# Transformer layer on one core: the last memory product, the first half's sums, the ahead products and the turned rows become steps of the planned list, and eight pairs run ahead

## The chip, the cores and the metric

One core of one Trainium2 chip runs the kernel. Its engines are named as the profile names them: PE (TensorE, matrix products and transposes, which are products with the identity), DVE (VectorE), ACT (ScalarE), POOL (GpSimd), SP (SyncE, which issues most DMAs). The metric is the device time of one execution in microseconds; less is better.

## The reference

One layer on 1024 rows of 1024 features in float32: two attention groups with an output projection, attention into 256 memory rows, and a feed forward with squared ReLU, each with an RMS norm before and after it and a residual sum. The parts around the change, cut from the reference:

```python
h = rmsnorm(x, g_mem_pre[l])
...
y = memory_cross_attention(h, mem_n, w_mq[l], w_mk[l], w_mv[l], w_mo[l])
x = x + rmsnorm(y, g_mem_post[l])
h = rmsnorm(x, g_ff_pre[l])
y = jnp.square(jax.nn.relu(h @ w_ff1[l])) @ w_ff2[l]
x = x + rmsnorm(y, g_ff_post[l])
```

`memory_cross_attention` ends with `o @ w_mo`; these are the memory products below.

## The kernel before

**How numbers are kept.** Each float32 operand of a product is split into a hi piece (a copy in a narrower form, made on ACT) and a lo piece (the rest, made by a subtraction on DVE or POOL). `mm3` (line 172) makes one product from three matmuls: hi by hi (L174), lo by hi (L175), hi by lo (L176). A weight block is thus loaded (SP), copied (ACT, L336), subtracted (DVE, L341, or POOL, L344) and only then used.

**How products are tiled.** A large product over two by two blocks is made from seven block products and sums of blocks. For the memory output the seven are listed in `MO` (L210); the last has the name A22. Each is made for two halves of the rows (rows 0 to 3 and rows 4 to 7, a row being 128 rows of x), in two pieces of weights (kp) and for two rows (tp). Their results are added in `ym` (`leave`, L1642), multiplied by the gain g_mem_post, normed and added to x (`close_row`, L1152: the inverse root `rm` on POOL, L1122 and L1123, then the close on DVE, L1163). The feed forward makes 16 pairs of blocks of hidden features (NP), each pair by seven products: `px`, `py`, `pz`, `pv`. The first half's rows, turned, are h3T; the second half's rows are turned on PE (trx, L2096), and sums and differences of the two halves, T1 to T4, are formed with B22 (class `Turn`, L2082).

**What sets the order.** Up to L1949 a planner, `Flow` (L56), issues the work. Streams of steps for PE are tried in a fixed order; a step is taken when its condition holds, and its cost moves a modelled clock. Work for the other engines is put into a list for each engine with the earliest time, a cost and a level; of what can start, the lowest level goes first. `Stock` (L269) puts the loads and splits of weight blocks into the same lists, up to some blocks ahead. The planner runs while the kernel is built; on the chip each engine takes its instructions in the order so made, and an instruction that waits holds all that stand behind it on that engine.

From L1966 on the order is written out by hand: the eight sums `xf` of hi and lo pieces of h3T on POOL (L2076), the loads and splits of the first blocks of w_ff1 (`split_ahead`, L2052), the second half's A22 product (L2172 on), the closes of its rows 6 and 7 (`row_out`, `row_sum`), four units of transposes and sums (`units[...].turn()`, `.sums()`, `.low()`), and between them the ahead products: for AHEAD = 7 pairs the first row, px and py, which need the first half's rows alone (`ahead`, L2060). Their results go to DRAM (p1d) and are read again when the pair's turn comes in the loop over the 16 pairs (`reload`). Just ahead of the loop stand the block sums of pair 0 (`cur.sums`, L2228 to L2235) and the splits of them, v0 and s1a.

## Time and profile before

| | before |
|---|---|
| median of 3 runs | 1468.5 us |
| lowest, highest | 1467.78 us, 1469.2 us |
| the profiled execution | 1469.17 us |
| its span | 1467.4 us |
| mean granted PE clock in it | 0.994 |

The times agree within 1.4 us. The span is that from the first to the last instruction of the profiled execution; its own time is 1.8 us longer. Rows of the profile give a line of the kernel, the operation, and "out<-in" by the program's names without numbers: `ym<-whimo,A22h` is a matmul of the last memory product, `trx<-ident,ym` a transpose of the second half's rows, `xf<-h3T_hi,h3T_lo` one of the eight sums. The time in square brackets is that for which the engine stood before the instruction, with what released it.

### The profile page before, as it was taken

The page shows a single profiled execution, that of the slowest core. Times are in us where ns is not written, and L with a number is a line of the kernel's source. Part 1 is how long each engine was busy: PE and PEld are TensorE (multiplying, and loading weights), DVE is VectorE, ACT ScalarE, POOL GpSimd, SP SyncE. Part 2 cuts the span into 40 slices and gives each one's busy share as a digit, 9 for nine tenths or more (in the row PEclk, how much of TensorE's full clock was granted, in tenths as well). Part 3 has the DMA queues.
Part 4 walks back from the last instruction along what each step waited for, and adds up shares of the span by engine and source line. Part 5 has one row for each costly group of instructions (what it writes and reads, how often), then busy time and mean ns, then how long its engine had stood idle before and what let it go on. Part 6 is the DMA issues. An engine that isn't in the chain of part 4 may idle for free.

```text
span 1467.4 us, 20996 instructions
## 1 busy us (share of the span) xinstructions
PE 1437.7 (98%) x7188; PEld 1213.0 (83%) x7188; DVE 980.7 (67%) x1678; ACT 865.8 (59%) x1542; POOL 474.5 (32%) x515
## 2 busy tenths in 40 slices
PE   9999999999999999999999699999999999999997
PEld 9888888888889978888787588888888888888886
DVE  5567778868677436785879787765555656655576
ACT  7457776667577755577787565545555443444442
POOL 1345555445435361343444703343232000000021
PEclk9999999999999999999999899999999999999999
DMA  8234677954546884454346557764444785345565
GB/s 332 72 94 103 137 171 180 278 127 111 130 111 190 275 311 158 146 199 129 130 130 201 183 201 250 246 217 158 152 149 166 282 320 182 137 152 189 189 241 201
DMA packets 102699, 268.89 MB, mean 183 GB/s; under 512 B 12968, under 2 KB 25520, under 8 KB 102592
## 3 DMA queue, kind: packets, MB, share of 16 engines
q1 hardware_dynamic: 97840, 259.16, 53.0%
q0 software_dynamic: 4608, 8.39, 3.9%
q8 instruction: 56, 0.92, 0.3%
q14 instruction: 51, 0.42, 0.1%
q10 hardware_dynamic: 144, 0.00, 0.0%
HBM read 187.23 MB, written 80.27 MB: 182 GB/s over the span
## 4 chain that ended last, share of the span: by engine, by line
PE 87%; DVE 4%; DMA 3%; ACT 2%; POOL 2%; issue 1%; SPq 0%; DVEq 0%; POOLq 0%; ACTq 0%
PE fx L176 4%; PE pv L654 4%; PE fx L174 4%; PE fx L175 4%; PE ptr L604 4%; PE px L174 3%; PE px L175 3%; PE px L176 3%; PE fy L176 3%; PE fy L174 3%; PE fy L175 3%; PE q L174 2%; PE q L175 2%; PE q L176 2%; PE pz L174 2%; PE pz L175 2%
## 5 line engine op out<-in xcount | busy, mean ns | idle before, releaser
L610 DVE TENSOR_TENSOR p<-ptr,p 128x512 fp32r<-128x512 f32 (+1 forms) x152 | 92.3, 616 | 32.5 <-ACT p L613 31.4
L2453 POOL TENSOR_SCALAR rf<-sf,e 128x1 f32<-128x1 f32 x8 | 8.6, 1069 | 323.9 <-ACT jf L2438 323.9
L2339 ACT ACTIVATE whif<-ra 128x1024 fp32r<-128x1024 f32 x37 | 39.3, 1061 | 125.4 <-PE fy L175 62.6
L613 ACT ACTIVATE p<-ptr 128x512 fp32r<-128x512 f32 (+1 forms) x152 | 79.7, 538 | 43.7 <-PE ptr L604 42.8
L2341 DVE TENSOR_TENSOR wlof<-ra,whif 128x1024 fp32r<-128x1024 f32 x37 | 45.3, 1225 | 88.0 <-ACT whif L2339 88.0
L654 PE MATMUL pv<-p,vs 128*128 128x512 f32 (+1 forms) x304 | 86.2, 371 | 0.4 <-DVE p L610 0.4
L2228 POOL TENSOR_TENSOR sc<-wf,wf 128x512 f32<-128x512 f32 x14 | 20.9, 1493 | 143.7 <-DMA wf<-in_w_ff 95.3
L174 PE MATMUL fx<-vhif,whif 128*128 128x512 f32 x168 | 65.4, 389 | 0.0
L176 PE MATMUL fx<-vhif,wlof 128*128 128x512 f32 x168 | 65.4, 389 | 0.0
L175 PE MATMUL fx<-vlof,whif 128*128 128x512 f32 x168 | 65.4, 389 | 0.0
L654 PEld LDWEIGHTS pv<-p,vs 128*128 128x128 f32 x304 | 53.0, 189 | 8.8 <-DVE p L610 0.8
L174 PE MATMUL k<-hT_hi,whik 128*128 128x512 f32 x128 | 52.8, 412 | 0.0
L174 PE MATMUL yw<-whiwo,yT_hi 128*128 128x512 f32 x128 | 50.4, 394 | 0.7 <-ACT yw L1215 0.7
L174 PE MATMUL q<-hT_hi,whiq 128*128 128x512 f32 x128 | 51.0, 398 | 0.0
L176 PE MATMUL k<-hT_hi,wlok 128*128 128x512 f32 x128 | 50.3, 393 | 0.0
L175 PE MATMUL k<-hT_lo,whik 128*128 128x512 f32 x128 | 50.2, 392 | 0.0
L175 PE MATMUL q<-hT_lo,whiq 128*128 128x512 f32 x128 | 50.1, 391 | 0.0
L176 PE MATMUL q<-hT_hi,wloq 128*128 128x512 f32 x128 | 50.0, 391 | 0.0
L176 PE MATMUL yw<-whiwo,yT_lo 128*128 128x512 f32 x128 | 49.9, 390 | 0.0
L175 PE MATMUL yw<-wlowo,yT_hi 128*128 128x512 f32 x128 | 49.8, 389 | 0.0
L174 PE MATMUL fy<-vhif,whif 128*128 128x512 f32 x128 | 49.8, 389 | 0.0
L175 PE MATMUL fy<-vlof,whif 128*128 128x512 f32 x128 | 49.8, 389 | 0.0
(740 smaller groups left out, 5078.1 us busy)
## 6 DMA issues: line engine op xcount, KB each, us to landing
ra<-gd SPq DMA_DIRECT2D x56, 512.0 KB, 3.5
wg<-in_w_ff SPq DMA_DIRECT2D x56, 512.0 KB, 4.7
wf<-in_w_ff SPq DMA_DIRECT2D x38, 512.0 KB, 4.1
gd<-s SPq DMA_DIRECT2D x48, 256.0 KB, 2.1
od<-ot SPq DMA_DIRECT2D x64, 128.0 KB, 2.9
od<-od POOLq DMA_DIRECT2D x32, 256.0 KB, 5.2
wrawmo<-wtT SPq DMA_DIRECT2D x16, 512.0 KB, 3.4
gd<-u SPq DMA_DIRECT2D x32, 256.0 KB, 2.4
```

Source lines behind the costliest of these rows:

```text
L174: nc.tensor.matmul(ps, lh, rh, start=start, stop=False, skip_group_check=more)
L175: nc.tensor.matmul(ps, lh, rl, start=False, stop=False, skip_group_check=more)
L176: nc.tensor.matmul(ps, ll, rh, start=False, stop=stop, skip_group_check=more)
L604: nc.tensor.transpose(tr[:, m, :], sp[:, k * P:(k + 1) * P], ident)
L610: flow.put("V", at, 0.56 if dead else 0.7, lambda: nc.vector.tensor_sub(pl[:, live, :], tr[:, live, :], f(ph[:, live, :])), done)
L613: flow.put("S", flow.end, 0.49 if dead else 0.6, lambda ph=ph, tr=tr, live=live: nc.scalar.activation(ph[:, live, :], tr[:, live, :], AF.C ...
L654: nc.tensor.matmul(pv[:, :, q0 * P:(q0 + k1 - k0) * P], v, x[:, :, k0:k1, :].rearrange("p m k q -> p m (k q)"), start=c == 0 and m == 0, s ...
L2228: eng.tensor_sub(sc[:, k1], r0[:, k0], r1[:, k0])
L2339: nc.scalar.activation(ah, ra, AF.Copy)
L2341: nc.vector.tensor_sub(al, ra, f(ah))
L2453: nc.gpsimd.tensor_scalar(r, ssf[b][:, 0:1], ssf[b][:, 1:2], e3[:, b:b + 1], op0=ALU.add, op1=ALU.add)
```

## The change

The list that `Flow` runs now reaches to the loop over the pairs. `product_quarters` makes all seven products for both halves. The sums `xf` are put into POOL's list at its last level, once h3T is complete and the attention's outputs are done. The ahead products of pairs 0 to 5 are steps of the stream of products (`first_rows`, named pf), their weights are blocks of `Stock`, and the transposes with their sums are a stream of their own (`unit_steps`, `unit`). AHEAD becomes 8; pairs 6 and 7 are still written by hand behind the list, with the last lows of T3 and T4 and the splits of pair 0. The hi pieces of mo and ff weights are put at ACT's first level. The four multiplications by the gain in each half that POOL did are done by DVE. The block sums of pair 0 go from DVE to POOL, and `Rows` loads the residual rows of all eight rows.

```diff
+            self.blocks += [(("ff", j), t["w_ff1"][j].rearrange("p a b -> p (a b)"), [P, D]) for j in range(8)]
...
+            self.home.update({("ff", j): "w" if j > 5 else ("w", "wq")[j % 2] for j in range(8)})
...
+                        flow.put(eng, at, 1.22, lambda: self.lo(key, e), last, 0 if key[0] in ("mo", "ff") else 1)
...
-                flow.put("S", flow.now, 1.06, lambda key=key: self.hi(key), halves, 2)
+                flow.put("S", flow.now, 1.06, lambda key=key: self.hi(key), halves, 0 if key[0] in ("mo", "ff") else 2)
...
-            self.left = [("w", n) for n in range(TB)] + [("m", n) for n in range(6)]
+            self.left = [("w", n) for n in range(TB)] + [("m", n) for n in range(8)]
...
-        for p, (a, _) in enumerate(MO[:7 - th]):
+        for p, (a, _) in enumerate(MO):
...
-        if th:
-            lasts.append(X)
...
-                flow.chain(at, [("S", 0.65, square(y[:, cs])), ("G", 1.6, lambda: nc.gpsimd.tensor_tensor(
-                    y[:, cs], y[:, cs], gains["memo"][:, cs], op=ALU.mult))] if p < 5 else [
-                        ("S", 0.65, square(y[:, cs])), ("V", 0.7, gained(y[:, cs]))],
+                flow.chain(at, [("S", 0.65, square(y[:, cs])), ("V", 0.7, gained(y[:, cs]))],
...
+        seen["outs"] = flow.end
...
+        yield from first_rows()
...
+        yield 0.0, lambda: there(*(("h3", "T", 0, a, k) for a in (0, 2) for k in range(0, KC, 2))) and "outs" in seen
+        h = acts["h3", 0]
...
+        for i in range(4):
+            for a in range(2):
+                h1s[i, a] = px.tile([P, HT], F32, tag="xf", bufs=8, name=f"xf{i}{a}")
+                s = (slice(None), slice(None), slice(a * 256, a * 256 + 256))
+                flow.put("G", flow.now, 1.25, lambda i=i, a=a, s=s: nc.gpsimd.tensor_add(
+                    h1s[i, a].rearrange("p (k n) -> p k n", k=2), f(h.h[i][s]), f(h.l[i][s])), None, 3)
...
+        h = acts["h3", 0]
+        for j in range(AHEAD - 2):
+            if j == 5:
+                yield 0.0, lambda: not stock.to_load and free["raw"].ready(2)
+                for k in range(2):
+                    pair0.append(wp.tile([P, D], F32, tag="wraw", bufs=3, name=f"wf{k * NP}"))
+                    nc.sync.dma_start(pair0[k], t["w_ff1"][k * NP].rearrange("p a b -> p (a b)"))
+            for part in range(2):
+                tag = ("s", "mm")[part]
+                yield (2.724, lambda: there(("ff", j)) and spare_tiles and free[tag].ready() and (part or free["t2"].ready(2)))
+                free[tag].take()
...
+                ps = mm_tile([P, HT], f"pf{j}{part}", tag)
+                wh, wl = stock.w["ff", j]
+                for kc in range(4):
+                    c = slice(part * HT + kc * P, part * HT + kc * P + P)
+                    i = part * 2 + kc // 2
+                    mm3(ps, wh[:, c], wl[:, c], h.h[i][:, kc % 2, :], h.l[i][:, kc % 2, :], kc == 0, kc == 3)
+                if part == 0:
+                    p1, g11 = short(f"p1_{j}"), short(f"g11_{j}")
+
+                    def kept(at, j=j, p1=p1):
+                        free["s"].give(at)
+                        flow.put("D", at, 0.7, lambda: nc.sync.dma_start(p1d[j][:, 0, :], p1))
+
+                    flow.put("S", flow.end, 0.6, lambda p1=p1, ps=ps: nc.scalar.activation(p1, ps, AF.Copy), kept, 0)
+                    continue
+                stock.done(("ff", j))
+
+                def added(at, j=j, g11=g11):
+                    free["mm"].give(at)
+                    flow.put("D", at, 0.7, lambda: nc.sync.dma_start(p1d[j][:, 1, :], g11),
+                             lambda end: [free["t2"].give(end + 2.5) for _ in range(2)])
+
+                flow.put("V", flow.end, 0.7, lambda p1=p1, g11=g11, ps=ps: nc.vector.tensor_add(g11, ps, p1), added, 0)
+
+    def unit_steps():
...
+            a, i = un.a, un.i
...
+                                 and free["t2"].ready(2) and (a or free["u4"].ready(10)))
+            for _ in range(2):
+                free[bk].take()
...
+            if a == 0:
...
+        d1, d4 = h1s[i, a], h1s[i + 2, a]
+        b12, b22 = un.src
...
+            for j in range(2):
...
+        def parts(n, src, level=1):
+            def go(at):
+                flow.put("S", at, 0.55, lambda: lows.__setitem__(n, un.hi(n, src)),
+                         lambda end: late.append(lambda: lows[n]()) if a and n in ("T3", "T4") else flow.put("V", end, 0.7, lambda: lows[n](), lowered, 2), level)
+            return go
+
+        def second(at):
+            parts("T1", d1)(at)
+            flow.put("V", at, 0.82, lambda: un.less(d2, b22, g22, d1), third, 0)
+
+        def third(at):
+            parts("T2", d2, 0)(at)
+            flow.put("V", at, 0.65, lambda: nc.vector.tensor_sub(d4, d2, d4), parts("T4", d4), 1)
+
+        flow.put("V", at, 0.82, lambda: un.less(d1, b12, g12, d1), second, 0)
+        flow.put("S", at, 0.82, scaled, lambda at: flow.put(
+            "V", at, 0.82, lambda: un.less(c12, b22, g22, c12), lambda end: (left(end), parts("T3", c12)(end)), 0), 0)
+        flow.put("S", at, 0.82, lambda: lows.__setitem__("B22", un.hi("B22", b22, g22)),
+                 lambda at: flow.put("V", at, 0.82, lambda: lows["B22"](), left, 0), 0)
 
...
-    EARLY = 3
-    xf = {}
-    for i in range(4):
-        for a in range(2):
-            xf[i, a] = pr.tile([P, HT], F32, tag="xf", bufs=8, name=f"xf{i}{a}")
-            s = (slice(None), slice(None), slice(a * 256, a * 256 + 256))
-            nc.gpsimd.tensor_add(xf[i, a].rearrange("p (k n) -> p k n", k=2),
-                                 f(h3[0].h[i][s]), f(h3[0].l[i][s]))
-    for j in range(EARLY):
-        split_ahead(j, ff1_raw(j), j == 0)
+    p2ys = ExitStack()
...
-    for b in (2, 3):
-        residual_in(b)
-    raws = {}
-    for tp in range(2):
-        ps, c = lasts[0][tp], slice(tp * P, tp * P + P)
-        for kp in range(2):
-            ah, al = quarters[1, "A22"]
-            wh, wl = stock.w["mo", 1, 6, kp]
-            for j in range(2):
-                mm3(ps, ah[:, kp * 2 + j, c], al[:, kp * 2 + j, c], wh[:, j, :], wl[:, j, :], False, kp == 1 and j == 1, True)
-        row_out(2 + tp, ps)
-    for b in range(3):
-        raws[EARLY + b] = ff1_raw(EARLY + b)
-    units = [Turn(a, i) for a in range(2) for i in range(2)]
-    add = {}
-    units[0].turn()
-    units[0].sums()
-    add[0] = ahead(0)
-    row_sum(2)
-    units[0].low()
-    add[0]()
-    row_sum(3)
...
-    p2s.close()
...
-    split_ahead(3, raws.pop(3))
-    units[1].low()
...
-    add[2] = ahead(2)
...
+        free["wq"].give(flow.now)
+        gains["mix"] = gain(p2, t["g_mix_post"], "g_mix_post")
+        rows_in = Rows()
+        flow.pumps[1] = rows_in.pump
+        flow.run([memory_out_steps(), memory_turn_steps(), memory_sums(), rstd_steps(1, (1,)), second_rows(), unit_steps(),
+                  second_filler()], lambda: stock.to_load or stock.to_split or rows_in.left)
...
-    cur, nxt = Weights(0), Weights(1)
-    cur.load(0)
-    cur.load(1)
-    add[3] = ahead(3)
-    units[2].low()
-    add[3]()
-    split_ahead(5, raws.pop(5))
-    units[3].turn()
-    add[4] = ahead(4)
-    units[3].sums()
-    add[4]()
-    units[3].low(1)
     saved = {}
...
 
+    def from_stock(j):
+        h = HiLo.__new__(HiLo)
...
+
...
+    cur, nxt = Weights(0), Weights(1)
+    cur.raw = dict(enumerate(pair0))
     reload(0)
-    split_ahead(6, raws.pop(6))
+    cur.sums()
+    cur.sum4()
     nxt.load(0)
     nxt.load(1, True)
-    cur.sums(nc.vector)
-    cur.sum4(nc.vector)
-    add[5] = ahead(5)
+    add = {}
+    add[6] = ahead(6)
+    add[7] = ahead(7)
     cur.split("s23")
-    units[3].low(2)
-    add[5]()
-    add[6] = ahead(6)
+    add[6]()
+    late[0]()
+    late[1]()
     cur.split("s1a")
-    units[3].low()
-    add[6]()
+    add[7]()
+    late[2]()
+    late[3]()
```

Three places of the order. On POOL, around the inverse roots of the second half's rows (rm40 is that of row 4; xf the sums; ssm the sums of squares). Before:

```order
L2076 TENSOR_TENSOR xf21_9572<-h3T0_hi2_9175,h3T0_lo2_9179 128x512
L2076 TENSOR_TENSOR xf30_9574<-h3T0_hi3_9176,h3T0_lo3_9180 128x512
L2076 TENSOR_TENSOR xf31_9576<-h3T0_hi3_9176,h3T0_lo3_9180 128x512
L1122 TENSOR_SCALAR rm40_9476<-ssm10_9081 128x1
L1123 TENSOR_TENSOR rm40_9476<-rm40_9476,mhalf_81 128x1
L1122 TENSOR_SCALAR rm50_9479<-ssm11_9082 128x1
L1123 TENSOR_TENSOR rm50_9479<-rm50_9479,mhalf_81 128x1
```

After:

```order
L1723 TENSOR_TENSOR xf10_9551<-h3T0_hi1_9283,h3T0_lo1_9287 128x512
L1723 TENSOR_TENSOR xf11_9552<-h3T0_hi1_9283,h3T0_lo1_9287 128x512
L1124 TENSOR_SCALAR rm60_9616<-ssm12_9143 128x1
L1125 TENSOR_TENSOR rm60_9616<-rm60_9616,mhalf_81 128x1
L1124 TENSOR_SCALAR rm70_9623<-ssm13_9144 128x1
L1125 TENSOR_TENSOR rm70_9623<-rm70_9623,mhalf_81 128x1
L1124 TENSOR_SCALAR rm40_9648<-ssm10_9141 128x1
L1125 TENSOR_TENSOR rm40_9648<-rm40_9648,mhalf_81 128x1
L1124 TENSOR_SCALAR rm50_9652<-ssm11_9142 128x1
L1125 TENSOR_TENSOR rm50_9652<-rm50_9652,mhalf_81 128x1
L1723 TENSOR_TENSOR xf20_9553<-h3T0_hi2_9284,h3T0_lo2_9288 128x512
```

The roots of rows 4 and 5 stood behind all eight sums; now those of four rows stand between the fourth and the fifth sum.

On PE, from the last matmuls of the last memory product (ym101) on; a line of "..." leaves out matmuls. Before:

```order
L176 MATMUL ym101_9086<-whimo_1_6_1_9462,A22l1_8851 128x512
L2096 MATMUL trx00_9644<-ident_76,ym10_9077 128x128
L2096 MATMUL trx00_9644<-ident_76,ym11_9078 128x128
...
L2096 MATMUL trx02_9649<-ident_76,ym10_9077 128x128
...
L174 MATMUL px0_9683<-h3T0_hi0_9173,wah0_9580 128x512
L175 MATMUL px0_9683<-h3T0_lo0_9177,wah0_9580 128x512
```

After:

```order
L176 MATMUL ym101_9146<-whimo_1_6_1_9538,A22l1_8913 128x512
L174 MATMUL pf00_9598<-h3T0_hi0_9282,whiff_0_9564 128x512
L175 MATMUL pf00_9598<-h3T0_lo0_9286,whiff_0_9564 128x512
L176 MATMUL pf00_9598<-h3T0_hi0_9282,wloff_0_9565 128x512
...
L174 MATMUL pf01_9628<-h3T0_hi2_9284,whiff_0_9564 128x512
...
L174 MATMUL pf10_9658<-h3T0_hi0_9282,whiff_1_9587 128x512
...
L174 MATMUL pf11_9684<-h3T0_hi2_9284,whiff_1_9587 128x512
...
L2069 MATMUL trx00_9713<-ident_76,ym10_9137 128x128
L2069 MATMUL trx00_9713<-ident_76,ym11_9138 128x128
```

The transposes of rows 4 and 5 followed the product directly; now both rows of pairs 0 and 1, 48 matmuls, stand between.

On DVE, ahead of the loop (v0lo and wlo_s1a are lo pieces of pair 0's blocks, g11 the first row's sums, T lows of the turned rows). Before:

```order
L2230 TENSOR_TENSOR sc0_9999<-wf16_9885,wf0_9883 128x512
L2235 TENSOR_TENSOR sd0_10003<-wf0_9883,sc0_9999 128x512
L2016 TENSOR_TENSOR v0lo_s230_10035<-sc0_9999,v0hi_s230_10034 128x1024
L2108 TENSOR_TENSOR T1_lo1_9761<-xf11_9568,T1_hi1_9760 128x2x256
L2108 TENSOR_TENSOR T3_lo1_9767<-c12_11_9966,T3_hi1_9766 128x2x256
L2048 TENSOR_TENSOR g11_5_10033<-py5_10018,p1_5_10031 128x512
L2016 TENSOR_TENSOR wlo_s1a0_10073<-wf16_9885,whi_s1a0_10072 128x1024
L2108 TENSOR_TENSOR T4_lo1_9770<-xf31_9576,T4_hi1_9769 128x2x256
L2048 TENSOR_TENSOR g11_6_10071<-py6_10056,p1_6_10069 128x512
```

After:

```order
L2166 TENSOR_TENSOR v0lo_s230_10106<-sc0_10037,v0hi_s230_10105 128x1024
L2198 TENSOR_TENSOR g11_6_10075<-py6_10060,p1_6_10073 128x512
L2081 TENSOR_TENSOR T3_lo0_9841<-c12_10_9932,T3_hi0_9840 128x2x256
L2081 TENSOR_TENSOR T3_lo1_9845<-c12_11_9945,T3_hi1_9844 128x2x256
L2166 TENSOR_TENSOR wlo_s1a0_10115<-wf16_9955,whi_s1a0_10114 128x1024
L2198 TENSOR_TENSOR g11_7_10104<-py7_10089,p1_7_10102 128x512
L2081 TENSOR_TENSOR T4_lo0_9871<-xf21_9554,T4_hi0_9870 128x2x256
L2081 TENSOR_TENSOR T4_lo1_9876<-xf31_9556,T4_hi1_9875 128x2x256
```

The sums of pair 0 (sc0, sd0) are gone from DVE. v0lo now comes after pair 6 and 7's products, with g11_6 and both T3 lows between it and wlo_s1a.

## The prediction

> **What bounds the kernel now.** First the page's busy times, then the waits of PE, then the time around the seam in windows and engine by engine.

> ```profile
> PE 1437.7 (98%) x7188; PEld 1213.0 (83%) x7188; DVE 980.7 (67%) x1678; ACT 865.8 (59%) x1542; POOL 474.5 (32%) x515
> PE trx L2096 <- DVE ym L1163: 11.0, 2, 9.4
> PE ym L175 <- DVE wlomo L341: 2.6, 4, 1.2
> PE px L174 <- DVE ym L2155: 0.9, 1, 0.9
> PE ym L174 <- ACT whimo L336: 0.4, 1, 0.4
> ```

> PE is busy 98% of a span of 1467.4 us: a change that leaves its instructions alone, as this one does, can win at most the 29.7 us in which it stands, and only where it stands or runs slowly. The rows of waits (us, count, longest) name the place: 11.0 + 0.9 us before the turned rows and the first ahead product, 2.6 + 0.4 us before weights of the second half's memory products. The windows (length, busy and count by engine, granted clock, DMA share, GB/s) add the speed:

> ```profile
> 800.00:820.00 20.00, 18.04 (x87) 14.71 (x87) 16.93 (x22) 15.02 (x29) 5.98 (x7) 1.00 0.73 264
> 820.00:840.00 20.00, 9.76 (x39) 6.77 (x37) 17.41 (x11) 6.81 (x10) 19.72 (x12) 0.89 0.26 79
> 835.00:840.00 5.00, 0.00 (x0) 0.00 (x0) 2.81 (x2) 0.00 (x0) 4.72 (x5) 0.58 0.00 0
> 840.00:846.00 6.00, 3.30 (x11) 2.44 (x12) 3.10 (x5) 4.83 (x12) 3.67 (x10) 0.50 0.84 281
> 860.00:1400.00 540.00, 540.00 (x2390) 446.97 (x2390) 331.54 (x375) 265.33 (x364) 84.34 (x60) 1.00 0.57 198
> ```

> From 820 to 840 PE works 9.76 us while POOL works 19.72; then the clock is 0.50 to 846, and from 860 to 1400 PE is full at a clock of 1.00. On PE's timeline (start, length, line, count, idle before) the seam reads:

> ```profile
> 830.41 0.39 PE L176 MATMUL ym<-whimo,A22l 128*128 128x512 f32 x1
> 840.19 0.45 PE L2096 MATMUL trx<-ident,ym 128*128 128x128 f32 x1 [9.39 <-DVE ym L1163]
> 842.22 1.75 PE L2096 MATMUL trx<-ident,ym 128*128 128x128 f32 x7 [1.58 <-DVE ym L1163]
> 844.90 0.79 PE L174 MATMUL px<-h3T_hi,wah 128*128 128x512 f32 x1 [0.93 <-DVE ym L2155]
> 849.60 0.39 PE L176 MATMUL px<-h3T_hi,wal 128*128 128x512 f32 x1
> 852.59 1.04 PE L2096 MATMUL trx<-ident,ym 128*128 128x128 f32 x8
> 853.38 0.48 PE L174 MATMUL px<-h3T_hi,whi_a 128*128 128x512 f32 x1
> ```

> Why it waits, on POOL and DVE:

> ```profile
> 820.96 16.72 POOL L2076 TENSOR_TENSOR xf<-h3T_hi,h3T_lo 128x512 f32<-128x512 f32 x8
> 837.78 0.29 POOL L1122 TENSOR_SCALAR rm<-ssm 128x1 f32<-128x1 f32 x1
> 840.29 0.55 POOL L1123 TENSOR_TENSOR rm<-rm,mhalf 128x1 f32<-128x1 f32 x1
> 838.76 1.28 DVE L1163 SCALAR_TENSOR_TENSOR ym<-ym,rm,xtm 128x1024 f32<-128x1024 f32 x1 [2.19 <-POOL rm L1123]
> 840.88 1.28 DVE L1163 SCALAR_TENSOR_TENSOR ym<-ym,rm,xtm 128x1024 f32<-128x1024 f32 x1 [0.83 <-POOL rm L1123]
> ```

> Eight sums of 2.1 us each (16.72 / 8) stand on POOL ahead of two inverse roots of under a microsecond; the roots release the closes of rows 4 and 5 on DVE, the closes the transposes. And no ahead product can run, since the transposes stand in front of them.

> **The change, part by part.** *The seam.* The last product's last matmul starts at 830.41; thirteen full-speed matmuls take 852.59 - 849.60 = 2.99 us, 0.23 each, so its slot ends at 830.64. Full speed is back at 849.60: 18.96 us. In them lie 8 transposes (853.38 - 852.59 = 0.79) and 11 matmuls (2.53), together 3.3. **Lost: 15.6 us**, 11.9 of it standing, 3.7 at half clock. In the new order four ahead products (pf00 to pf11, 4 x 12 x 0.23 = 11.0 us) stand between the last memory product and the first transposes, and the four inverse roots stand behind four of the sums, not eight. Neither wait remains as it is, so I take off all 15.6 and then count what is late next. *The weight waits*, 2.6 + 0.4 = **3.0 us**, go as they are too, since hi pieces of these weights now come first on ACT; what takes their place is the next term.

> *DVE up to the transposes.* What is late next hangs on DVE. Its prices:

> ```profile
> 785.05 1.28 DVE L1648 TENSOR_TENSOR ym<-ym,g_mem_post 128x512 f32<-128x512 f32 x2
> 808.92 2.35 DVE L341 TENSOR_TENSOR wlomo<-wrawmo,whimo 128x1024 fp32r<-128x1024 f32 x2
> 811.20 3.22 DVE L1281 SCALAR_TENSOR_TENSOR h3T_lo<-tr_h3T,gf,h3T_hi 128x256 fp32r<-128x256 f32 x8
> 820.40 3.92 DVE L341 TENSOR_TENSOR wlomo<-wrawmo,whimo 128x1024 fp32r<-128x1024 f32 x2 [1.80 <-ACT whimo L336]
> 832.09 4.48 DVE L2016 TENSOR_TENSOR wlo_a<-wf,whi_a 128x1024 fp32r<-128x1024 f32 x2
> ```

> From the second half's first product (784, where both programs are still alike) to the close of row 5, the new order has on DVE 17 weight lows at 1.17, 25 ops of 128x512 at 0.64 (14 gains, 6 adds, 4 lows of sums, 1 first-row add), 6 closes at 1.28 and 16 turned lows at 0.40: 19.9 + 16.0 + 7.7 + 6.4 = 50 us. PE comes to the first transposes at 830.64 - 3.0 + 11.0 = 838.6 if nothing waits: 54.6 us. Beside the sums, though, two lows took 3.92 and 4.48 and not 2.35: 3.7 us more over four lows beside some four sums (8.4 us / 2.1), 0.9 for each sum. Four sums make 3.6: DVE's work is 53.6 of 54.6 us. It fits with nothing to spare, and an order kept for so long will meet some waits. Bounds: nothing, or the old 3.0 and all that is added (8 gains moved from POOL at 0.64 = 5.1), 8.1. By the walk through the order, the lows of the fourth product's second piece come some 0.7 us late (turned lows stand before them), those of the last product 1.3, the first ff block 0.3, the closes of rows 4 and 5 another 0.8. **3.1 us**, nearer to the 3.0 of the row than to the sum. Each is short, so full clock: the wait of 1.20 below left it at 1.00 in 800:820.

> ```profile
> 807.86 0.50 PE L175 MATMUL ym<-wlomo,S1h 128*128 128x512 f32 x1 [1.20 <-DVE wlomo L341]
> ```

> The closes of rows 6 and 7 come four products (11.0 us) later with room: **0**, and if DVE lags, their wait is in rival 2.

> *The entry of the loop.* The rest of the hand-written part stands behind pair 7's products now.

> ```profile
> 884.86 1.06 ACT L2013 ACTIVATE v0hi_s<-sc 128x1024 fp32r<-128x1024 f32 x1 [2.86 <-DVE sc L2230]
> 885.96 1.23 DVE L2016 TENSOR_TENSOR v0lo_s<-sc,v0hi_s 128x1024 fp32r<-128x1024 f32 x1 [0.40 <-ACT v0hi_s L2013]
> 885.83 0.58 ACT L2046 ACTIVATE p<-px 128x512 f32<-128x512 f32 x1
> 887.70 0.68 DVE L2108 TENSOR_TENSOR T_lo<-c,T_hi 128x512 fp32r<-128x512 f32 x1
> 888.90 1.21 DVE L2016 TENSOR_TENSOR wlo_s1a<-wf,whi_s1a 128x1024 fp32r<-128x1024 f32 x1
> 891.13 0.39 PE L176 MATMUL pz<-T_hi,wlo_s1a 128*128 128x512 f32 x1
> 898.72 1.66 DVE L2016 TENSOR_TENSOR wlo_s1a<-wfu,whi_s1a 128x1024 fp32r<-128x1024 f32 x1
> 890.58 1.29 POOL L2228 TENSOR_TENSOR sc<-wf,wfu 128x512 f32<-128x512 f32 x1 [33.94 <-DMA wfu<-in_w_ff]
> 899.38 2.16 POOL L2229 TENSOR_TENSOR wf<-wf 128x512 f32<-128x512 f32 x1
> ```

> From the end of px7: the copy of p1 on ACT (0.58) and v0hi (1.06) make 1.7; v0lo (1.2) makes 2.9, needed by px0's third matmul 12 + 2 matmuls on, at 14 x 0.23 = 3.2. Then g11_6, T3_lo0, T3_lo1 (0.65 each) and wlo_s1a (1.21) make 6.1; pz0's third matmul needs it at 26 x 0.23 = 6.0. No margin, and v0lo also frees POOL's sums of pair 1, which before ran later (890.58). Beside such a sum wlo_s1a took 1.66 and not 1.2, the sum 2.16 and not 1.29. Three DVE ops each 0.5 (as there) to 1.29 (a whole sum) longer give 1.3 to 3.7 us of wait; with no overlap none. I take **2.0**, near the row's 0.5 each. g11_7 and the late lows come after wlo_s1a; pv0 reads them 24 matmuls later: 0.2 for these.

> *What lies beside other work.* Pair 7's first row ahead adds two stores and a reload, and one add on DVE in place of an ACT copy; in the window 860:1400 PE stands nowhere, so the loop can neither gain nor, unless a new wait arises there, lose: 0. The sums of pair 0 go from DVE to POOL (four of 1.29 to 2.16, some 7 us), which stood 33.94 us there: 0.

> ```profile
> wf<-in_w_ff SPq DMA_DIRECT2D x38, 512.0 KB, 4.1
> ```

> SP issues the eight ff loads earlier, and loads of two more rows, past the stores of the first half's rows; they land 4.1 us after issue and fall into 820:840, where DMA was at 0.26. ff0's raw buffer comes free with the last products' lows, so a late one would show as a wait before pf, of up to 4.1 us: I take 0, and it lies in the range.

> *Sum*, against the profiled execution (1469.17 us): - 15.6 - 3.0 + 3.1 + 2.0 + 0.2 = - 13.3, 1455.9. The median of the runs shown is 0.67 below that execution: **1455.2**. Own range: 1469.17 - 0.67 - 18.6 = 1449.9 with no new wait, and with 8.1 + 3.7 + 1.5 for the rest 1463.2.

> **Rivals.**
> 1. *DVE becomes the bound through the seam.* All it is given is paid: 5.1 us of gains and 8 sums x 0.9 = 7.2, 12.3 of new waits, at the transposes and at the weights of pf. For it: 53.6 of 54.6 us. Against it: from 838 on DVE has fewer weights to lower, and four products stand before each group of transposes. 1469.17 - 18.6 + 12.3 - 0.67 = 1462.2.
> 2. *A sum and a DVE op block each other for a whole length.* Then each of the four sums up to the transposes costs DVE 1.29 (a sum alone, as at 890.58) and not 0.9, 1.6 in all, and the entry waits 3.7 and not 2.0. 1455.2 + 1.6 + 1.7 = 1458.5. For it: both ops at 898 grew. Against it: 1.66 is 0.45 above 1.21, not 1.29.
> 3. *Almost nothing waits.* Waits come to 1 us, because the list puts weights that are due ahead of gains and closes: 1469.17 - 18.6 + 1.0 - 0.67 = 1450.9. Against it: the entry, whose order is written by hand.
> 4. *Slower.* DVE's lag of rival 1, 12.3 us, falls in two long waits, before the 16 transposes of rows 4 and 5 and before those of rows 6 and 7, behind which all products are queued, and each halves the clock, as 9.39 us did here (0.58, then 0.50; 3.7 us lost): 12.3 + 7.4 + 2.0 at the entry = 21.7 against 18.6, 1471.6. It decides where each of the two waits is long enough to halve the clock; 1.20 was not, 9.39 was. Against it: 11.0 us of products before each group, in which DVE can catch up.

> That the change doesn't do what it says is ruled out by the order, which shows the products ahead of the transposes and the roots ahead of half the sums.

> [...]

> **Chances.** Forecast 0.53, rivals in their order 0.15, 0.15, 0.11, 0.06. The range 1449.5 to 1463.5 takes in the bounds above and all but rival 4 and the upper ends of rival 1. A difference under 0.2% (2.9 us) is about what a measurement here can't tell from none. Faster by more than that 0.90; within it 0.04, from between rivals 1 and 4; slower 0.06, rival 4.

> **What would show it.** Right: the row of trx waits gone or under 1.5 us, clock 1.00 in every window from 820 to 860, pf rows directly behind the last ym row, wlo_s1a with 1 to 3 us of idle before pz. Wrong: trx or pf waits over 4 us with a clock under 0.9; DVE at 20 of 20 us from 820 to 860 (rival 1); waits on DMA ahead of pf; or a wait after 900, where I count none.

## The result and the profile after

| | before | changed |
|---|---|---|
| median (runs) | 1468.35 us (4) | 1449.99 us (4) |
| lowest to highest | 1467.78 to 1469.2 us | 1449.56 to 1450.85 us |
| profiled execution, span | 1469.17, 1467.4 us | 1449.93, 1448.0 us |
| ratio, 95% interval | | 0.9875 [0.9858, 0.9892] |

The changed kernel is 18.4 us faster; 13.3 were forecast. Its page shows PE busy for 4.6 us less with the same 7188 matmuls, its waits hold one new row, and its windows show where PE is not full:

```profile
PE 1433.1 (99%) x7188; PEld 1211.2 (84%) x7188; DVE 977.8 (68%) x1684; ACT 864.5 (60%) x1540; POOL 470.8 (33%) x511
PE px L174 <- DVE g L2198: 2.2, 1, 2.2
820.00:840.00 20.00, 20.00 (x98) 16.68 (x97) 17.16 (x23) 13.70 (x26) 14.90 (x16) 1.00 0.77 245
840.00:860.00 20.00, 20.00 (x98) 16.78 (x97) 19.70 (x34) 13.58 (x27) 5.20 (x5) 1.00 0.59 218
860.00:880.00 20.00, 17.66 (x70) 13.70 (x69) 20.00 (x26) 11.44 (x18) 10.34 (x7) 0.91 0.51 185
```

The rows for trx, for wlomo and for whimo are gone from the waits; PE is full at a clock of 1.00 from 820 to 860, where it worked 9.76 of 20 us before. What is left lies from 860 to 880, and there DVE works 20.00 of 20 us. On the timelines of DVE and PE the first group of transposes reads:

```profile
829.41 1.28 DVE L1165 SCALAR_TENSOR_TENSOR ym<-ym,rm,xtm 128x1024 f32<-128x1024 f32 x1 [1.47 <-POOL rm L1125]
832.34 2.32 DVE L1165 SCALAR_TENSOR_TENSOR ym<-ym,rm,xtm 128x1024 f32<-128x1024 f32 x1
834.62 1.96 PE L2069 MATMUL trx<-ident,ym 128*128 128x128 f32 x16
782.00:834.60 52.60, 52.60 (x248) 43.63 (x247) 48.36 (x64) 39.82 (x73) 26.18 (x29) 1.00 0.76 259
```

The close of row 5 ends at 834.66, the transposes start at 834.62 with no idle time noted: the row is there at the moment when PE comes to it. DVE worked 48.36 of the 52.60 us up to it (the window's row).

At the entry of the loop, PE, then two of the sums of pair 0 on POOL, then DVE:

```profile
870.68 0.39 PE L176 MATMUL py<-h3T_hi,wloff 128*128 128x512 f32 x1
873.27 0.47 PE L174 MATMUL px<-T_hi,v0hi_s 128*128 128x512 f32 x1 [2.20 <-DVE g L2198]
874.83 0.63 PE L174 MATMUL px<-T_hi,v0hi_s 128*128 128x512 f32 x1
878.45 0.50 PE L176 MATMUL pz<-T_hi,wlo_s1a 128*128 128x512 f32 x1
878.79 0.39 PE L174 MATMUL pz<-T_hi,whi_s1a 128*128 128x512 f32 x1
874.50:878.40 3.90, 3.81 (x10) 2.54 (x8) 3.90 (x3) 1.05 (x2) 2.74 (x2) 0.56 0.22 84
...
865.71 1.62 POOL L2242 TENSOR_TENSOR sc<-wf,wf 128x512 f32<-128x512 f32 x1
867.40 1.63 POOL L2247 TENSOR_TENSOR sd<-wf,sc 128x512 f32<-128x512 f32 x1
864.82 3.06 DVE L1812 TENSOR_TENSOR xf<-T,xf 128x512 f32<-128x512 f32 x2
867.80 1.78 DVE L2081 TENSOR_TENSOR T_lo<-T,T_hi 128x512 fp32r<-128x512 f32 x1
871.31 1.21 DVE L2166 TENSOR_TENSOR v0lo_s<-sc,v0hi_s 128x1024 fp32r<-128x1024 f32 x1
872.45 0.68 DVE L2198 TENSOR_TENSOR g<-py,p 128x512 f32<-128x512 f32 x1
873.05 3.13 DVE L2081 TENSOR_TENSOR T_lo<-c,T_hi 128x512 fp32r<-128x512 f32 x2
876.10 2.30 DVE L2166 TENSOR_TENSOR wlo_s1a<-wf,whi_s1a 128x1024 fp32r<-128x1024 f32 x1
```

py7's last slot ends at 870.68 + 0.23 = 870.91. px0's first product (12 matmuls) and three matmuls of pz0 would be over 15 x 0.23 = 3.4 us later, at 874.3; pz0's fourth starts at 878.79. **The entry loses 4.5 us**: 2.2 of it standing before px0, for the sum g11 of pair 6, the rest matmuls at a clock of 0.56. The next section asks which of these is the cause.

The account from the first memory product of the first half on (731.01 us in the profile of before, 728.81 in that of the changed kernel) to the end is 736.4 us before and 719.2 after, 17.2 less: 15.6 at the seam; 4.7 before it, where the 444 matmuls from that first one to the last of the memory products take 99.40 us before and 94.69 after (the profile of before notes 3.0 of idle time there for weights of these products); 4.5 given back at the entry; and 1.3 behind the last matmul, which stands 8.0 us from the end before and 6.7 after. These make 17.1; the 0.1 that is missing is within what this count of slots resolves. The 2.2 us ahead of that first product are dealt with under the repeated run below.

### The profile page after: what moved, and what is told of

It is laid out like the page before. It is cut to its first block, busy times and chain, and to the rows that moved or that the text cites. A ratio compares the mean times of both kernels' runs of the same rounds, so it can differ in the third digit from the quotient of the medians.

```text
span 1448.0 us, 20982 instructions
## 1 busy us (share of the span) xinstructions
PE 1433.1 (99%) x7188; PEld 1211.2 (84%) x7188; DVE 977.8 (68%) x1684; ACT 864.5 (60%) x1540; POOL 470.8 (33%) x511
## 4 chain that ended last, share of the span: by engine, by line
PE 92%; DVE 4%; ACT 2%; DMA 1%; issue 1%; SPq 0%; DVEq 0%; POOLq 0%; POOL 0%; ACTq 0%
PE pv L656 4%; PE fx L175 4%; PE fx L176 4%; PE fx L174 4%; PE ptr L606 4%; PE fy L175 3%; PE fy L174 3%; PE fy L176 3%; PE px L174 2%; PE px L176 2%; PE px L175 2%; PE q L174 2%; PE pz L176 2%; PE q L175 2%; PE q L176 2%; PE pz L174 2%
## 5 line engine op out<-in xcount | busy, mean ns | idle before, releaser
L174 PE MATMUL fx<-vhif,whif 128*128 128x512 f32 x168 | 65.4, 389 | 0.0
L175 PE MATMUL fx<-vlof,whif 128*128 128x512 f32 x168 | 65.4, 389 | 0.0
L176 PE MATMUL fx<-vhif,wlof 128*128 128x512 f32 x168 | 65.4, 389 | 0.0
L174 PE MATMUL k<-hT_hi,whik 128*128 128x512 f32 x128 | 52.8, 412 | 0.0
L174 PE MATMUL q<-hT_hi,whiq 128*128 128x512 f32 x128 | 51.0, 398 | 0.0
L174 PE MATMUL yw<-whiwo,yT_hi 128*128 128x512 f32 x128 | 50.4, 394 | 0.1
L176 PE MATMUL k<-hT_hi,wlok 128*128 128x512 f32 x128 | 50.2, 392 | 0.0
L175 PE MATMUL k<-hT_lo,whik 128*128 128x512 f32 x128 | 50.2, 392 | 0.0
L175 PE MATMUL q<-hT_lo,whiq 128*128 128x512 f32 x128 | 50.1, 391 | 0.0
L176 PE MATMUL q<-hT_hi,wloq 128*128 128x512 f32 x128 | 50.0, 391 | 0.0
L176 PE MATMUL yw<-whiwo,yT_lo 128*128 128x512 f32 x128 | 49.9, 389 | 0.0
L175 PE MATMUL yw<-wlowo,yT_hi 128*128 128x512 f32 x128 | 49.8, 389 | 0.0
L174 PE MATMUL fy<-vhif,whif 128*128 128x512 f32 x128 | 49.8, 389 | 0.0
L175 PE MATMUL fy<-vlof,whif 128*128 128x512 f32 x128 | 49.8, 389 | 0.0
## 6 DMA issues: line engine op xcount, KB each, us to landing
ra<-gd SPq DMA_DIRECT2D x56, 512.0 KB, 3.7
wg<-in_w_ff SPq DMA_DIRECT2D x56, 512.0 KB, 4.9
wf<-in_w_ff SPq DMA_DIRECT2D x31, 512.0 KB, 3.8
wrawmo<-wtT SPq DMA_DIRECT2D x16, 512.0 KB, 3.5
```

What stands on the lines that cost most here:

```text
L174: nc.tensor.matmul(ps, lh, rh, start=start, stop=False, skip_group_check=more)
L175: nc.tensor.matmul(ps, lh, rl, start=False, stop=False, skip_group_check=more)
L176: nc.tensor.matmul(ps, ll, rh, start=False, stop=stop, skip_group_check=more)
```

## Experiments

Each is the changed kernel with one edit; "changed" below is 1449.99 us, and 1451.16 where it ran again. The kernel before gave 1468.11 to 1468.77 us beside them.

### Order on PE or order on POOL

Two things went at once: products came between the last memory product and the transposes, and the roots came ahead of half of the sums. Three kernels undo the one, the other and both.

```diff
# e1: a step of first_rows also needs the transposes of rows 4 and 5
+                yield (2.724, lambda: "turned4" in seen and there(("ff", j)) and spare_tiles and free[tag].ready() and (part or free["t2"].ready(2)))
...
+                seen["turned4"] = flow.end
# e2: the sums at POOL's first level
+                    h1s[i, a].rearrange("p (k n) -> p k n", k=2), f(h.h[i][s]), f(h.l[i][s])), None, 0)
# e3: both
```

> The ahead products wait in the list until the transposes of rows 4 and 5 are issued; the sums on POOL stay as changed, four ahead of the roots and four behind. Theory A (the products between the last memory product and the transposes took the loss away): PE stands 8 to 10 us before trx and the clock halves after it, 10 to 13.5 us more than the changed kernel, 1460 to 1463.5 us. Theory B (the roots no longer standing behind eight sums took it away): the roots come as early as now, at most 3 us more, 1450 to 1453 us.

> The eight sums go at POOL's first level, so all stand ahead of the four roots; PE's products still stand ahead of the transposes, six of them now. Theory A: nothing to be seen, 1449 to 1451 us, no wait before trx. Theory B: the roots are late again, trx waits 4 us or more and the clock halves, 1455 us or more.

> Both undone at once: transposes behind the last product, eight sums ahead of the roots. Theory A: as with the transposes alone put first, within 2 us of that run, since the sums now start at once when h3T is there and are done before the sums of squares are. Theory B: the whole loss is back, 15 us and more, 1465 us or more, and well above the run with the transposes alone.

Medians: **1466.44** (1464.87 to 1468.16), **1453.42** (1453.0 to 1454.43), **1468.09** (1465.9 to 1469.28). The waits of PE in e1, in e3 (with its first root on POOL) and in e2:

```profile
PE trx L2070 <- DVE ym L1165: 10.6, 2, 6.9
PE pf L174 <- DVE g L1767: 2.0, 1, 2.0
PE pz L176 <- DVE wlo_s1a L2167: 1.8, 1, 1.8
...
PE trx L2070 <- DVE ym L1165: 11.8, 2, 10.2
828.36 1.40 POOL L1124 TENSOR_SCALAR rm<-ssm 128x1 f32<-128x1 f32 x1 [0.36 <-ACT junk L1117]
...
PE px L174 <- DVE g L2198: 3.3, 1, 3.3
PE pf L176 <- DVE wloff L343: 0.7, 1, 0.7
```

With the transposes alone put first, 10.6 us of waits before them are back, although the roots come as early as in the changed kernel, and nearly the whole gain is gone. That is theory A; it gave 1460 to 1463.5, since it left out what then comes late behind (2.0, 1.8 us and 0.9 before px). With the sums alone put first, no wait before trx is seen, and the long wait of theory B does not come; the time lies in neither range. This does not show the place of the sums to be free: the list put six products there and not four, and the close of row 5 ends at 839.75 us, while the transposes, at 843.03, would have stood at 837.6 without the two more products (24 matmuls of 0.227). The 2 to 3 us that e2 loses stand elsewhere: 0.7 before a pf, and at the entry, where PE waits 3.3 and not 2.2. Its first group of transposes comes two products later, so DVE has less time up to the entry; that this shift is the reason was not tried by itself. With both, the waits before trx are 11.8 instead of 10.6 us and the time is that of the kernel before, 1.7 us above e1. The sums do not stand in the way of the roots there: they are done 0.36 us before the first root, which waits for ACT.

### Gains and the level of the hi pieces

```diff
# e4: gains of p < 5 on POOL again
-                flow.chain(at, [("S", 0.65, square(y[:, cs])), ("V", 0.7, gained(y[:, cs]))],
+                flow.chain(at, [("S", 0.65, square(y[:, cs])), ("G", 1.6, lambda: nc.gpsimd.tensor_tensor(
+                    y[:, cs], y[:, cs], gains["memo"][:, cs], op=ALU.mult))] if p < 5 else [
+                        ("S", 0.65, square(y[:, cs])), ("V", 0.7, gained(y[:, cs]))],
# e5: hi pieces of mo and ff at ACT's third level again
+                flow.put("S", flow.now, 1.06, lambda key=key: self.hi(key), halves, 2)
```

> The four gains in each half go back to POOL. Theory of slack (DVE had room up to the transposes, the forecast's 3.1 us for it were wrong): 1449 to 1451 us, no wait before trx or pf. Theory that the move was needed: gains of 1.3 to 2.5 us each stand ahead of the roots on POOL, trx waits 1 to 4 us, 1451.5 to 1455 us.

> The hi pieces of mo and ff weights go back to ACT's third level. Theory P (that level took the waits for weights of the memory products away, 5.2 us with what each costs beside its idle time): waits of ym or pf on whimo, wlomo, whiff or wloff come back, 2 to 5 us in all, 1452 to 1455 us. Theory Q (they went because the list with more blocks in it places them otherwise): no such waits, 1449 to 1451 us.

Medians: **1453.89** (1453.02 to 1454.82) and **1462.57** (1461.08 to 1464.0). e4 falls into the range of "the move was needed", but not by its wait: no trx waits; 0.9 us stand before a pf, 1.3 and 1.4 before px at the entry. Its profiled execution stood longer far ahead of the seam; from the first memory product on it takes 1.8 to 2.4 us more than the two profiles of the changed kernel, so less than the 3 to 4 us is the edit's. In e5 theory P is right in kind and too small (12.6 us were lost, 2 to 5 expected):

```profile
PE ym L175 <- DVE wlomo L343: 4.1, 3, 2.3
PE pf L174 <- DVE g L1767: 2.4, 1, 2.4
PE pf L174 <- ACT p L1758: 1.9, 1, 1.9
PE pz L176 <- DVE wlo_s1a L2166: 1.8, 1, 1.8
```

The 4.1 us and 0.9 for whimo are the weight waits of before, and larger; what comes behind costs as much again. One number, the level of the hi pieces, carries some 12 us.

### What the entry waits for

e6 moves one line (the sum g11 of pair 6 ahead of v0's split). e7 and e10 put the differences T4 of rows 6 and 7 behind the entry's lows; e10 also reorders them.

```diff
# e6
+    add[6]()
     cur.split("s23")
-    add[6]()
# e7 (and e10): T4 of the second rows behind
+            if a:
+                behind.append((un, d2, d4))
...
-    late[2]()
-    late[3]()
+    for un, d2, d4 in behind:
+        nc.vector.tensor_sub(d4, d2, d4)
+        un.hi("T4", d4)()
# e10: the order at the entry
     add[6] = ahead(6)
+    add[6]()
+    cur.split("s23")
     add[7] = ahead(7)
-    cur.split("s23")
-    add[6]()
+    cur.split("s1a")
     late[0]()
     late[1]()
-    cur.split("s1a")
     add[7]()
```

> On DVE the sum g11 of pair 6, for which px0 waited 2.2 us, goes ahead of v0's low. Theory C (the end of DVE's queue, wlo_s1a, bounds the entry; the wait before px0 and the half clock behind it only lie in its shadow): px0 starts about a microsecond earlier, pz0's third matmul where it was, 1449.5 to 1450.7 us. Theory D (the wait before px0 with its half clock is the loss): 2 to 3.5 us less, 1446.5 to 1448 us.

> The two differences T4 of rows 6 and 7, which took 3.06 us on DVE beside POOL's sums, go with their pieces behind the entry's lows. Theory C: wlo_s1a comes 3 us earlier, the entry loses 1.3 to 1.6 us and not 4.6, 1446.4 to 1447.6 us, with a wait of about 1.3 us before px0 left. Theory D: g11 stays behind v0's low, so the wait before px0 stays 1 to 2 us and the clock halves all the same, 1448.5 to 1450 us.

> T4 of rows 6 and 7 behind the entry, g11 of pair 6 ahead of v0's low, v0 split ahead of pair 7's products on ACT, and wlo_s1a ahead of the lows of T3. Both theories: next to nothing is left to wait for at the entry, 4 us and more gained, 1445.5 to 1446.5 us; if a wait is left it is before pv0, for T4, or before B22's products, for u0.

Medians: **1450.11** (1449.7 to 1451.3), **1453.04** (1451.41 to 1454.04), **1453.34** (1451.64 to 1454.88). e6 has the time of theory C, but not its signs. The wait before px0 and the half clock are gone (1.00 in the windows from 860 to 900), and pz0's third matmul, which theory C had unmoved, stands 146.8 us behind the first memory product and not 149.6; 1.4 of that go again in a wait for u. From the first memory product to the end e6 takes 717.9 us, against 719.2 in the changed kernel's profile and 718.7 in that of its repeated run below: some 1 us is won, which the times do not resolve. Part of what moved is not the edit's (see the sums on POOL below), so e6 does not decide between C and D. e7 and e10 miss every number: wlo_s1a did come early and PE did not wait there, but for a sum (u) that reads px0's first product and that now stood behind T4 on DVE. First e6, then e7, then e10:

```profile
PE px L174 <- DVE u L2384: 1.4, 1, 1.4
PE px L176 <- DVE v0lo_s L2166: 0.6, 1, 0.6
PE pz L176 <- DVE wlo_s1a L2166: 0.4, 1, 0.4
...
PE px L174 <- DVE u L2388: 3.4, 1, 3.4
...
PE px L174 <- DVE u L2388: 4.1, 1, 4.1
```

So two more were made, each with px0's first product and its sum u2 written ahead of the loop: e11 with T4 behind, e12 with T4's differences where the list put them and only the lows of T4 behind u2. The changed kernel ran again beside them.

```diff
# e12, at the entry (e11: as e10, with the same lines from "x = bank" on, then T4)
+    add[6]()
     cur.split("s23")
-    add[6]()
+    cur.split("s1a")
     late[0]()
     late[1]()
-    cur.split("s1a")
     add[7]()
...
+    x = bank("px0")
+    product(x, cur.w["s23"], 0, XT["T2"])
...
+    nc.vector.tensor_add(u2_0, x, p1)
...
     late[2]()
     late[3]()
```

> The changed kernel as it is, once more. It says how far one profiled execution of it stands from another: 1449.5 to 1451 us; the wait before px0 2.2 us and the half clock behind it again; the first memory product of the first half, at 728.81 us in the first profile and 731.01 in that of before, anywhere between 728.5 and 732, if its place is a matter of the execution and not of the change.

> As the run with the whole entry reordered, and with px0's first product and the sum u2 that reads it put ahead of the differences T4 on DVE, since there px0 stood 4.1 us for u2 behind them. Theory C (DVE's queue at the entry is the bound, and what stands ahead of what PE needs next decides): no wait of 1.5 us or more is left between 868 and 885, the clock stays full, 1445.8 to 1447.5 us. Theory E (the queue is too full whatever its order, a wait only moves on): a wait of 2 us or more before pv0 or B22's products, 1449 to 1451 us.

> T4's differences stay where the list put them, ahead of the entry's lows; g11 of pair 6 goes ahead of v0's low, wlo_s1a ahead of the lows of T3, and px0's first product with u2 ahead of the lows of T4. Theory C: waits of 0.6 us for v0's low, and of 1 to 2 us for u2, are left since 3 us of differences are still in front of them; the clock stays full; 1447.5 to 1449.5 us, between the changed kernel and the run with T4 moved. Theory E: as the changed kernel, 1449.5 to 1451 us.

Medians: changed again **1451.16** (1450.58 to 1452.55), e11 **1451.34** (1450.66 to 1455.26), e12 **1447.59** (1447.19 to 1448.58; 0.986 of before [0.9845, 0.9874]). Waits of the changed kernel again, of e11 and of e12:

```profile
PE pz L176 <- DVE wlo_s1a L2166: 1.7, 1, 1.7
PE px L174 <- DVE g L2198: 1.7, 1, 1.7
...
PE pz L174 <- DVE g L2421: 2.8, 1, 2.8
...
PE px L174 <- ACT u0hi_s L2163: 0.5, 1, 0.5
PE px L174 <- DVE u L2295: 0.4, 1, 0.4
PE px L176 <- DVE v0lo_s L2166: 0.3, 1, 0.3
```

In its second execution the changed kernel stands 1.7 us before px0 instead of 2.2, its clock stays at 1.00, and it stands another 1.7 before pz0's third matmul, for wlo_s1a: the half clock of the first execution only hid this wait. **What bounds the entry of the changed kernel is the end of DVE's queue.** e11 is theory E's wait (its time is 0.3 us above that range): T4 out of the way of u2, the next sum (g of pz0), which B22's products need, is late by 2.8, and the clock halves behind it (0.63 from 885.2 to 889). e12 is theory C's: nothing over 0.5 us is left, and it is 3.6 us faster than the changed kernel beside it. From the first memory product on it takes 716.6 us, against 719.2 and 718.7 in the two profiles of the changed kernel, so 2.1 to 2.6 us are the entry's. Both theories were too simple: a thing put behind makes the next late, unless each stands in the order in which PE asks for it. That is a matter of order more than of how full the queue is: in e10 DVE works only 16.82 of 20 us from 860 to 880, and in e11 it stands 1.68 us for ACT's hi piece of v0 and twice 0.70 for those of T4, with what PE needs behind. e12 has PE's order; its windows still have DVE at 20.00 of 20 us from 860 to 880.

The repeated run also settles the first 2.2 us of the account: its first memory product stood at 730.42 us, 1.6 later than in the first profile of the same program, and in the other kernels it stood between 728.80 and 731.87. It is a matter of the execution. The 1.3 us behind the last matmul are not explained: every kernel with the new code has 6.7 to 6.9 us there, and of the kernel before there is one profile.

### What POOL's sums cost DVE

```diff
# e9
+    cur.sums(nc.vector)
+    cur.sum4(nc.vector)
```

> The four sums of pair 0 go from POOL back to DVE, behind the lows of T1 and T2 and ahead of v0's low. Theory C1 (beside a sum on POOL the DVE op loses as much as the sum would cost DVE itself, 0.7 us each: 2.9 us over the four, seen as 3.06 for two differences and 1.78 for a low): DVE's queue ends where it ended, 1449.5 to 1451.7 us, and no DVE op from 860 to 872 is longer than it is alone. Theory C2 (the long ops there have another cause, the sums on POOL are nearly free): DVE's queue is 2.7 us longer, wlo_s1a later by that, 1452.5 to 1454.5 us.

Median **1450.99** (1450.46 to 1451.52): theory C1. wlo_s1a ends 150.0 us behind the first memory product, 149.6 in the changed kernel; PE stands 2.6 us before px0, now for ACT (p1r). DVE's ops at that place, with POOL idle until 874:

```profile
866.04 1.28 DVE L1812 TENSOR_TENSOR xf<-T,xf 128x512 f32<-128x512 f32 x2
867.24 0.68 DVE L2081 TENSOR_TENSOR T_lo<-T,T_hi 128x512 fp32r<-128x512 f32 x1
869.65 0.68 DVE L2240 TENSOR_TENSOR sc<-wf,wf 128x512 f32<-128x512 f32 x1
877.64 2.31 DVE L2166 TENSOR_TENSOR wlo_s1a<-wf,whi_s1a 128x1024 fp32r<-128x1024 f32 x1
```

The same three ops took 3.06 + 1.78 us beside the sums and take 1.28 + 0.68 without: 2.9 us, and the four sums take DVE 2.9 us when it makes them. Moving them to POOL freed DVE of nothing. wlo_s1a, still beside a sum of pair 1, keeps its 2.31.

It is not always DVE that is kept waiting. In e6, whose edit begins behind these ops, the third sum and the differences read:

```profile
866.29 4.89 POOL L2242 TENSOR_TENSOR sc<-wf,wf 128x512 f32<-128x512 f32 x1
866.34 1.28 DVE L1812 TENSOR_TENSOR xf<-T,xf 128x512 f32<-128x512 f32 x2
```

There the sum took 4.89 us and DVE's ops kept their lengths, but v0's hi piece came later for it, and DVE stood 1.68 us for that piece. In e11 the same sum took 3.60. What decides which of the two engines stands is not shown.

## Why the prediction came out as it did

The time fell into the range, 0.5 us above its lower end and 5.2 below the forecast, and near the number of rival 3, though not for its reason, since the entry did wait. Of the 5.9 us by which the profiled execution lies below its forecast (1455.9), the terms below account for 3.8; 2.2 are where its first memory product stood, which is luck.

- **The seam, - 15.6.** Right, and for the reason given: e1 brings the waits back by moving the transposes alone. The prediction named the sums on POOL as what made the closes late, and in the kernel before the roots do stand right behind them. But with the roots as early as in the changed kernel e1 still waits 10.6 us before trx: the gain needs the products between.
- **The weight waits, - 3.0.** Right in kind, too small: they cost 4.7 with the slots around each wait. (The 5.2 in the expectation of e5 is counted in the kernel before alone; the changed kernel loses some at such places too.) The prediction gave the level of the hi pieces half a sentence; e5 shows that without it the change would have won some 6 us.
- **DVE up to the transposes, + 3.1.** This step failed. It made 53.6 us of work in 54.6 and then took waits by hand from the order. Measured were 48.36 us of work in 52.60 and no wait at all: the count took whole lengths where ops follow each other more closely (0.64 and 1.28 for a pitch of 0.60 and 1.2), and charged 3.6 us for sums beside DVE work, where two of the 64 ops were longer, 1.7 us in all (a wlomo of 1.90 for 1.22, the close of row 5 of 2.32 for 1.28). It lay close, all the same: the close of row 5 came just when PE did.
- **The entry, + 2.0 and 0.2.** The mechanism was right, v0lo, T3's lows and then wlo_s1a behind them, beside POOL's sums, with no margin; the size was not, 4.5. The prediction priced the move of pair 0's sums to POOL at 0 because POOL stood idle there, and counted the path to v0lo as free of them. The move is worth nothing (e9), but the path was not free: the sums ran beside DVE ahead of v0lo and cost it 2.9 us.
- **Rival 1**, DVE as the bound through the seam, did not come, but behind the seam it did: 20.00 of 20 us from 860 to 880. **Rival 2** was near for the entry (3.7 there, where 4.5 went in the first execution and 1.7 + 1.7 of waits in the second) and not for the stretch before it. Beside a sum T_lo took 1.78 and not 0.68, wlo_s1a 2.30 and not 1.21, 1.1 more each, near the 1.29 of a sum alone and more than the 0.45 of the one row (1.66) on which the prediction weighed this rival. Rival 4 did not come.

Sum by what was measured, from the first memory product on: - 15.6 - 4.7 + 0 + 4.5 = - 15.8, with 1.3 behind the last matmul - 17.1, where 17.2 were measured.

## What to carry to other kernels

Where a group of instructions waits for a long chain on other engines, look first for work that is ready and stands behind it in the queue: putting four products ahead was worth more here than shortening the chain (without them e1 stood 10.6 us before trx, although its roots came early). When the wait is gone, read which engine is at 20 of 20 us next: there each op should stand in the order in which the bound engine asks for it (e12, 3.6 us faster), and moving one thing behind only moved the wait, until the whole order was right (3.4, 4.1 and 2.8 us in e7, e10 and e11). Work moved to an idle engine is not free if it slows the busy one beside it, as pair 0's four sums on POOL slowed DVE by 2.9 us: compare the lengths of the same op with and without it, on both engines.

## What was not expected of the hardware

```profile
867.20:870.61 3.41, 1.48 (x7) 0.90 (x5) 3.41 (x7) 0.60 (x1) 0.00 (x0) 1.00 0.00 0
870.61:874.02 3.41, 2.94 (x13) 2.44 (x14) 2.15 (x3) 0.11 (x1) 0.00 (x0) 1.00 0.54 198
...
867.90:871.31 3.41, 1.01 (x4) 0.67 (x4) 3.41 (x7) 0.60 (x1) 0.00 (x0) 1.00 0.00 0
871.31:874.72 3.41, 3.41 (x9) 2.63 (x8) 0.89 (x1) 0.00 (x0) 0.00 (x0) 0.50 1.01 315
```

The wait of e3 lies across two steps, with PE standing 1.9 us in the one and 0.5 in the other; that of e5 lies in one, 2.4 us. Over all steps of the fourteen profiles at full clock and ahead of the last matmul, the ten in which PE stood 2.1 us or more (2.08 to 3.41) were each followed by a step at half clock, and all others, with 1.94 us or less, by a full one. In these profiles, the place of a wait of 2 to 3 us among the steps thus went with whether the clock dropped; the first full stretch, from which they are counted, begins 6.31 us into the span of the kernel before and 4.20 into that of the changed one. Whether the kernel's order sets this place is not shown. Of the 2.20 us before px0 in the first profile of the changed kernel 2.08 lay in one step, the least of the ten; its second profile has no wait as long as that, and keeps its clock.

Nor did the drop come at once: px0's first matmuls after the wait still ran at full pitch (0.23 us), up to the end of the step at 874.60, and only then at 0.43.
